# A head pair's logits and its A@V as ordered chains, rope's squares in one instruction, and a query projection in two parts

## The chip, the cores and the metric

The kernel runs on one core of a Trainium2 chip. The time is that of one execution on the device, in microseconds (us); the median of three runs is used. Lower is better.

## What is computed

Four layers of a decoder trunk on 256 tokens of width 1024, in float32. Each layer has a token mixer (layer 0 and 3: stick-breaking attention; 1: MoBA, which at 256 tokens is causal attention within one block; 2: a sliding window of 128 with two key heads and a learned sink per head) and a SwiGLU channel mixer, each behind an RMSNorm that is modulated by a vector c. There are 16 heads of width 64. Cut to what matters here:

```python
def stick_breaking_attention(h, w_in, w_out):
    q, k, v = jnp.split(h @ w_in, 3, axis=-1)
    z = einsum('bhqd,bhkd->bhqk', q, k) * scale
    log_beta = log_sigmoid(z)
    log_keep = where(past, log_sigmoid(-z), 0.0)
    later = cumsum(log_keep, axis=3, reverse=True) - log_keep
    a = where(past, exp(log_beta + later), 0.0)
    return merge_heads(einsum('bhqk,bhkd->bhqd', a, v)) @ w_out

def swa_sink_attention(h, w_in, qk_gain, sinks, w_out, cos, sin):
    q = apply_rope(rms_norm(q, qk_gain[0]), cos, sin)
    k = apply_rope(rms_norm(k, qk_gain[1]), cos, sin)
    ...
    m = maximum(max(s, axis=-1), sink)
    e = exp(s - m)
    p = e / (sum(e, axis=-1) + exp(sink - m))
    return merge_heads(p @ vb) @ w_out

for i in range(DEPTH):
    h = modulate(rms_norm(x, norm_gain[i, 0]), sh1, sc1)
    x = x + g1 * mixer[i % 3](h)
    h = modulate(rms_norm(x, norm_gain[i, 1]), sh2, sc2)
    x = x + g2 * swiglu(h, w_gate, w_up, w_down)
```

## The kernel before, in words

The layers run one after the other, each as projection, attention over eight pairs of heads, output projection, FFN. Products in float32 are made from two halves: a value is split into a rounded part (`hi`, `qkh`, `oth`; made on ScalarE) and the rest (`lo`, `qkl`, `otl`; made by a subtraction on VectorE), and three matmuls (hi by hi, lo by hi, hi by lo) are added up in PSUM (`mm3` with 256 columns, `tt3` with 512). Weights stream in as 1 MB pieces (`raw`) and are split in the same way by `prep` (L218 and L219, two halves of 128x1024 each); between them the modulation weights are multiplied by c on VectorE (L176, also 128x1024). Both of these serve later work: they are queued ahead of need at a low priority, and may stand anywhere among the attention's instructions.

One pair of heads in attention goes as follows. `scores` takes two PSUM buffers of tag `z` (there are two in all), one per head. Into each goes the mask (`identb` times the mask, L516; L518 in the sliding window, with 384 columns), and on top six matmuls for the logits (L523): three products of halves, each once for the first 128 queries (256 columns) and once for the rest (128 columns). A head's rows are 64 of the 128, the other head's the other 64. The source writes these alternating between the two heads.

- Stick-breaking (`sb_layer`): ScalarE makes Abs, Exp, Ln and Relu of `z` (L595 to L599), VectorE scans in two pieces (L601) and subtracts from the logits (L602), which is the last reader of `z`; ScalarE makes the exponential (L603).
- The other two (`softmax`): VectorE takes the maxima (L671, L672) and makes the bias `nb`, ScalarE the exponentials (L685, L686, the last readers of `z`), in the sliding window also the sink's (`es`, L682) ahead of them; VectorE makes the reciprocal and scales, ScalarE scales the rest (L691).
- `apply_v`, for the pair before: three transposes a head (L454) into a buffer `at`, a copy `aT` on ScalarE (L456), four matmuls A@V (L462: two heads by 256 and 128 columns) into `po`, and the split of the result (L470, L471).

MoBA and the sliding window also apply RMSNorm and rope to queries and keys (`rope`): one Square per head with the sum in its accumulator (L645), then products with the tables on VectorE. In the sliding window the queries come in two halves of 512 columns; `proj_q(1)`, the second, stands between the first and second pair and uses PSUM tags `at` and `o`, with 24 matmuls for each of two blocks of 128 tokens.

`out_proj` adds up the output projection for the first seven pairs' results as they come (in bank `wo`), and these matmuls fill TensorE between the logits.

Every engine takes its instructions in program order. What that order is, is decided by the framework's scheduler, which places each instruction where its own estimate has operands and buffers ready; the source's order is only its priority. `follow` adds a dependency that costs nothing at run time but forces an order of two instructions on one engine (matmul after matmul).

## Time and profile before

| | |
|---|---|
| median of 3 runs | 1260.95 us (1259.98 to 1266.66) |
| the profiled execution | 1266.64 us, its span 1264.9 us |
| TensorE (PE) busy | 1235.1 us, 98% |
| VectorE (DVE) busy | 1012.1 us, 80% |
| ScalarE (ACT) busy | 717.4 us, 57% |
| mean granted TensorE clock | 0.99 of full |

Times of the trace are microseconds from the span's start. A line `L523` is that of the source before. "Idle before" is how long an engine had nothing to run ahead of an instruction, and behind the arrow stands what released it. Rows of matmuls may be merged and overlap: an instruction's duration contains the way through the array, so that steps are read from start to start. In a window's row the clock is what was granted to TensorE on average (1.00 is 2.4 GHz, 0.50 is 1.2 GHz).

### The profile page before, as it was taken

To read this page: it belongs to the slowest core of one execution; us is meant where nothing else is said; L and a number is where in the kernel's file an instruction comes from. 1 tells how busy PE (TensorE), PEld (TensorE's weight loads), DVE (VectorE), ACT (ScalarE), POOL (GpSimd) and SP (SyncE) were. 2 spreads that over 40 slices of the span, in tenths; PEclk is the share of its full clock that TensorE was granted. 3 is DMA by queue.
4 is the path that set the end of the run, shared out by engine and by line. 5 is a ranking of instruction groups with operands and counts; after the bars stand their busy time and mean duration, and the time that the engine had idled before them with its cause. 6 is when DMAs were issued, how large, how long until landed. Compare 5 with 4: busy or idle time off the path is not lost.

```text
span 1264.9 us, 23755 instructions
## 1 busy us (share of the span) xinstructions
PE 1235.1 (98%) x9546; PEld 1159.9 (92%) x9546; DVE 1012.1 (80%) x1909; ACT 717.4 (57%) x1455; POOL 6.2 (0%) x28
## 2 busy tenths in 40 slices
PE   7999999999999999999998999999999999999998
PEld 5878999999977799999996689999998889999998
DVE  7989999898798769989879669887869876966542
ACT  4578565454478756545448676444446776644531
POOL 0000000000000000000000000000000000000000
PEclk9989999999999999999999899999999999999999
DMA  9966779988644227999864007987865641676530
GB/s 367 364 251 237 265 267 402 360 324 329 253 172 161 101 82 276 394 349 340 330 232 167 34 34 257 348 334 289 295 242 208 242 149 68 258 269 210 196 117 18
DMA packets 44033, 303.35 MB, mean 240 GB/s; under 512 B 5009, under 2 KB 6801, under 8 KB 7442
## 3 DMA queue, kind: packets, MB, share of 16 engines
q1 hardware_dynamic: 43922, 301.83, 64.0%
q8 instruction: 75, 1.23, 0.4%
q14 instruction: 36, 0.29, 0.1%
HBM read 300.76 MB, written 1.05 MB: 239 GB/s over the span
## 4 chain that ended last, share of the span: by engine, by line
PE 85%; DVE 8%; ACT 4%; issue 1%; DMA 1%; SPq 0%; DVEq 0%; ACTq 0%
PE ps_wo L382 8%; PE ps_wo L383 8%; PE ps_wo L381 8%; PE ps_z L381 8%; PE ps_z L382 8%; PE ps_z L383 8%; PE ps_pj L381 4%; PE ps_pj L382 4%; PE ps_pj L383 4%; PE ps_at L382 3%; PE ps_at L381 3%; PE ps_at L383 3%; PE ps_o L462 3%; DVE lo L219 3%; PE ps_z L523 3%; DVE raw L176 2%
## 5 line engine op out<-in xcount | busy, mean ns | idle before, releaser
L219 DVE TENSOR_TENSOR lo<-raw,hi 128x1024 fp32r<-128x1024 f32 x378 | 454.6, 1220 | 100.8 <-ACT hi L218 100.1
L218 ACT CAST hi<-raw 128x1024 fp32r<-128x1024 f32 x378 | 387.0, 1049 | 209.4 <-issue 50.6
L176 DVE SCALAR_TENSOR_TENSOR raw<-raw,cact 128x1024 f32<-128x1024 f32 x192 | 229.4, 1217 | 5.7 <-DMA raw<-ada 5.7
L381 PE MATMUL ps_z<-hh,hi 128*128 128x256 f32 x736 | 206.1, 280 | 0.0
L382 PE MATMUL ps_z<-hl,hi 128*128 128x256 f32 x736 | 205.8, 280 | 0.0
L383 PE MATMUL ps_z<-hh,lo 128*128 128x256 f32 x736 | 204.8, 278 | 0.0
L381 PE MATMUL ps_wo<-ahi,hi 128*128 128x256 f32 x704 | 199.2, 283 | 0.0
L382 PE MATMUL ps_wo<-alo,hi 128*128 128x256 f32 x704 | 199.2, 283 | 0.0
L383 PE MATMUL ps_wo<-ahi,lo 128*128 128x256 f32 x704 | 199.2, 283 | 0.0
L381 PE MATMUL ps_pj<-hh,hi 128*128 128x256 f32 x512 | 146.7, 287 | 2.4 <-DVE qkl L530 2.4
L382 PE MATMUL ps_pj<-hl,hi 128*128 128x256 f32 x512 | 145.5, 284 | 0.0
L383 PE MATMUL ps_pj<-hh,lo 128*128 128x256 f32 x512 | 144.3, 282 | 0.0
L382 PEld LDWEIGHTS ps_z<-hl,hi 128*128 128x128 f32 x736 | 139.1, 189 | 0.0
L381 PEld LDWEIGHTS ps_z<-hh,hi 128*128 128x128 f32 x736 | 138.3, 188 | 0.0
L383 PEld LDWEIGHTS ps_z<-hh,lo 128*128 128x128 f32 x736 | 138.2, 188 | 0.0
L382 PEld LDWEIGHTS ps_wo<-alo,hi 128*128 128x128 f32 x704 | 135.2, 192 | 0.0
L383 PEld LDWEIGHTS ps_wo<-ahi,lo 128*128 128x128 f32 x704 | 135.2, 192 | 0.0
L381 PEld LDWEIGHTS ps_wo<-ahi,hi 128*128 128x128 f32 x704 | 135.1, 192 | 0.0
L381 PEld LDWEIGHTS ps_pj<-hh,hi 128*128 128x128 f32 x512 | 98.1, 192 | 4.1 <-DVE qkl L530 2.8
L382 PEld LDWEIGHTS ps_pj<-hl,hi 128*128 128x128 f32 x512 | 98.8, 193 | 0.7
L383 PEld LDWEIGHTS ps_pj<-hh,lo 128*128 128x128 f32 x512 | 98.0, 191 | 0.1
L381 PE MATMUL ps_at<-hh,hi 128*128 128x256 f32 x336 | 94.0, 280 | 0.0
(220 smaller groups left out, 2405.6 us busy)
## 6 DMA issues: line engine op xcount, KB each, us to landing
raw<-wst SPq DMA_DIRECT2D x189, 1024.0 KB, 5.5
raw<-ada SPq DMA_DIRECT2D x96, 1024.0 KB, 6.2
x<-xin SPq DMA_DIRECT2D x4, 256.0 KB, 4.4
out<-x SPq DMA_DIRECT2D x8, 128.0 KB, 1.7
mraw<-masks SPq DMA_DIRECT2D x1, 256.0 KB, 6.6
ropec<-ropec SPq DMA_DIRECT2D x2, 128.0 KB, 4.5
early<-small SPq DMA_DIRECT2D x1, 128.0 KB, 2.1
qkg<-qkg SPq DMA_DIRECT2D x2, 64.0 KB, 4.9
```

The source lines that it names most:

```text
L176: filler("v", nc.vector.scalar_tensor_tensor(raw[:, j * D : (j + 1) * D], raw[:, j * D : (j + 1) * D], 1.0, cact, ALU.mult, ALU.mult, accu ...
L218: filler("s", nc.scalar.copy(hi[:, cols], raw[:, cols]))
L219: filler("v", nc.vector.tensor_sub(lo[:, cols], raw[:, cols], hi[:, cols].bitcast(F32)))
L381: first = nc.tensor.matmul(ps, whi, ahi, start=start, stop=False, skip_group_check=True)
L382: nc.tensor.matmul(ps, whi, alo, start=False, stop=False, skip_group_check=True)
L383: nc.tensor.matmul(ps, wlo, ahi, start=False, stop=stop, skip_group_check=True)
L462: last = nc.tensor.matmul(po[rows, cols], vf(j, 2 * pair + hh_), ats[hh_][:, src], start=j == 1, stop=j == 0, skip_group_check=True)
L523: nc.tensor.matmul(z[:, out], q[a][rows, tq], k[b][rows, tk], start=False, stop=b == 1, skip_group_check=True)
```

## The change

A helper `in_order` forces a list of instructions into that order. It is applied to the fourteen matmuls of a pair's masks and logits, and to the four of A@V. Other matmuls may still stand between them. Rope's squares become one Square over all heads and a reduction on VectorE. `proj_q` of the sliding window is called for one block of tokens at a time; the second half's two blocks stand behind the first pair's and the second pair's logits, in PSUM tags `wo`, and the first A@V comes behind the second of them.

```diff
+    def in_order(instructions):
+        for a, b in zip(instructions, instructions[1:]):
+            follow(a, b)
...
+        av = []
         for j, cols, src in ((1, slice(0, S), slice(P, 3 * P)), (0, slice(0, P), slice(0, P))):
             for hh_ in range(2):
                 rows = slice(hh_ * HD, (hh_ + 1) * HD)
-                last = nc.tensor.matmul(
+                av.append(nc.tensor.matmul(
                     po[rows, cols], vf(j, 2 * pair + hh_), ats[hh_][:, src], start=j == 1, stop=j == 0, skip_group_check=True
-                )
+                ))
+        in_order(av)
+        last = av[-1]
...
         zs = [ptile("z"), ptile("z")]
+        row = []
         for z in zs:
...
-                nc.tensor.matmul(z[:, 0 : 3 * P], identb, mask, start=True, stop=False, skip_group_check=True)
+                row.append(nc.tensor.matmul(z[:, 0 : 3 * P], identb, mask, start=True, stop=False, skip_group_check=True))
...
-                    nc.tensor.matmul(z[:, out], q[a][rows, tq], k[b][rows, tk], start=False, stop=b == 1, skip_group_check=True)
+                    row.append(nc.tensor.matmul(z[:, out], q[a][rows, tq], k[b][rows, tk], start=False, stop=b == 1, skip_group_check=True))
+        in_order(row)
         return zs
...
-        for h in range(n):
-            nc.scalar.activation(sq3[:, h, :], s3[:, h, :], AF.Square, accum_out=ss[:, h : h + 1])
+        nc.scalar.activation(sq3, s3, AF.Square)
+        nc.vector.tensor_reduce(ss[:, :n], sq3, AX.X, ALU.add)
...
-        def proj_q(n, tags):
-            ps = half_proj(wbase + 1 + 2 * n, hh, hl, tags)
-            for j in range(2):
-                r = small.tile([P, 8], F32, tag="rq", name="rq")
-                q[j, n] = rope(ps[j], 8, tab, j, 0, r)
-                nc.vector.tensor_scalar_mul(qs[:, j, 8 * n : 8 * n + 8], r, QK_SCALE)
+        def proj_q(n, tags, j):
+            ps = half_proj(wbase + 1 + 2 * n, hh, hl, tags, (j,))[0]
+            r = small.tile([P, 8], F32, tag="rq", name="rq")
+            q[j, n] = rope(ps, 8, tab, j, 0, r)
+            nc.vector.tensor_scalar_mul(qs[:, j, 8 * n : 8 * n + 8], r, QK_SCALE)
...
-        proj_q(0, ("wo", "wo"))
+        wo = ("wo", "wo")
+        for j in range(2):
+            proj_q(0, wo, j)
         turn(0)
         turn(1)
-        weights(0)
-        proj_q(1, ("at", "o"))
-        for p in range(1, 8):
+        for p in range(8):
             weights(p)
-            finish(p - 1)
-            if p < 3:
+            if p < 2:
+                proj_q(1, wo, p)
+            if p:
+                finish(p - 1)
+            if p in (1, 2):
                 turn(p + 1)
         out_proj(l, wbase + 5, lambda: finish(7))
```

All lines shift by 5 to 12, so that L219 is L224 in the changed kernel, L601 is L611 and L523 is L532. The number of instructions stays the same on TensorE; ScalarE has 86 fewer and VectorE 14 more. Since the scheduler runs over the whole program, instructions that the diff does not name move too.

TensorE, MoBA, the sixth pair (its `z` are 5030 and 5031 before, 4982 and 4983 after; `at` are transposes for the pair before it, `wo` the output projection). Before:

```order
L516 MATMUL ps_z_5030<-maskb_105,identb_104 128x2x128
L523 MATMUL ps_z_5030<-qkh_4958 128x256
L523 MATMUL ps_z_5030<-qkh_4958 128x128
L523 MATMUL ps_z_5030<-qkh_4958,qkl_4959 128x256
L523 MATMUL ps_z_5030<-qkh_4958,qkl_4959 128x128
L523 MATMUL ps_z_5030<-qkl_4959,qkh_4958 128x256
L523 MATMUL ps_z_5030<-qkl_4959,qkh_4958 128x128
L454 MATMUL ps_at_5071<-ident_103,a_4983 128x128
L516 LDWEIGHTS identb_104
L516 MATMUL ps_z_5031<-maskb_105,identb_104 128x2x128
L523 MATMUL ps_z_5031<-qkh_4958 128x256
```

and after:

```order
L459 MATMUL ps_at_5023<-ident_103,a_4935 128x128 x2
L387 MATMUL ps_wo_5172<-otl_4591,hi_4818 128x256
L459 MATMUL ps_at_5023<-ident_103,a_4935 128x128
L388 MATMUL ps_wo_5172<-oth_4590,lo_4819 128x256
L386 MATMUL ps_wo_5173<-oth_4590,hi_4826 128x256
L387 MATMUL ps_wo_5173<-otl_4591,hi_4826 128x256
L525 LDWEIGHTS identb_104
L525 MATMUL ps_z_4983<-maskb_105,identb_104 128x2x128
L532 MATMUL ps_z_4982<-qkh_4910 128x256
L532 MATMUL ps_z_4983<-qkh_4910 128x256
L532 MATMUL ps_z_4982<-qkh_4910 128x128
L532 MATMUL ps_z_4983<-qkh_4910 128x128
```

The heads now alternate (the first head's mask stands four rows ahead of this piece), and the transposes that stood between the heads have moved ahead of the second mask.

VectorE, first stick-breaking layer, from the sixth pair (`a_1115`, `a_1125`) to the first scan of the seventh (`a_1214`); `lo` is half a weight split, `raw` a modulation product, `x2` two of them. Before:

```order
L601 SCALAR_TENSOR_TENSOR a_1115<-a_1115,e_1111 128x128
L601 SCALAR_TENSOR_TENSOR a_1125<-a_1125,e_1121 128x256
L602 SCALAR_TENSOR_TENSOR a_1115<-ps_z_1095,a_1115 128x384
L601 SCALAR_TENSOR_TENSOR a_1125<-a_1125,e_1121 128x128
L219 TENSOR_TENSOR lo_1345<-raw_1138,hi_1344 128x1024
L602 SCALAR_TENSOR_TENSOR a_1125<-ps_z_1096,a_1125 128x384
L471 TENSOR_TENSOR otl_1191<-ps_o_1173,oth_1190 128x256
L176 SCALAR_TENSOR_TENSOR raw_1134,mod_133<-raw_1134,cact_85 128x1024 x2
L601 SCALAR_TENSOR_TENSOR a_1214<-a_1214,e_1210 128x256
```

and after:

```order
L611 SCALAR_TENSOR_TENSOR a_1115<-a_1115,e_1111 128x128
L181 SCALAR_TENSOR_TENSOR raw_1338,mod_133<-raw_1338,cact_85 128x1024
L612 SCALAR_TENSOR_TENSOR a_1115<-ps_z_1095,a_1115 128x384
L611 SCALAR_TENSOR_TENSOR a_1125<-a_1125,e_1121 128x256
L611 SCALAR_TENSOR_TENSOR a_1125<-a_1125,e_1121 128x128
L479 TENSOR_TENSOR otl_1191<-ps_o_1173,oth_1190 128x256
L612 SCALAR_TENSOR_TENSOR a_1125<-ps_z_1096,a_1125 128x384
L540 TENSOR_TENSOR qkl_1255<-ps_pj_1148,qkh_1254 128x512
L224 TENSOR_TENSOR lo_1361<-raw_1342,hi_1360 128x1024 x2
L181 SCALAR_TENSOR_TENSOR raw_1350,mod_133<-raw_1350,cact_85 128x1024
L181 SCALAR_TENSOR_TENSOR raw_1354,mod_133<-raw_1354,cact_85 128x1024
L611 SCALAR_TENSOR_TENSOR a_1214<-a_1214,e_1210 128x256
```

Three of the big instructions stood there, and five stand there now; over the seven such stretches of this layer it is 4, 4, 3, 4, 4, 3, 5 before and 5, 5, 5, 5, 5, 5, 4 after.

ScalarE, sliding window, the sixth pair (its sinks' exponentials are `es_8601` before, `es_8529` after), with the copies for the pair before it (`aT`) and that pair's A@V evacuation (`oth`). Before:

```order
L456 COPY aT_8632<-ps_at_8628 128x384
L456 COPY aT_8638<-ps_at_8634 128x384
L682 ACTIVATE es_8601<-nb_8598,sinks_106 128x2
L685 ACTIVATE a_8603,sm_8604<-ps_z_8579,nb_8598,qscale_7937 128x256
L686 ACTIVATE a_8603,sm_8604<-ps_z_8579,nb_8598,qscale_7937 128x128
L682 ACTIVATE es_8617<-nb_8614,sinks_106 128x2
L685 ACTIVATE a_8619,sm_8620<-ps_z_8580,nb_8614,qscale_7937 128x256
L691 ACTIVATE a_8603<-a_8603,sm_8604 128x128
L686 ACTIVATE a_8619,sm_8620<-ps_z_8580,nb_8614,qscale_7937 128x128
L470 CAST oth_8644<-ps_o_8627 128x256
L691 ACTIVATE a_8619<-a_8619,sm_8620 128x128
```

and after:

```order
L461 COPY aT_8560<-ps_at_8556 128x384
L701 ACTIVATE a_8480<-a_8480,sm_8481 128x128
L461 COPY aT_8566<-ps_at_8562 128x384
L478 CAST oth_8572<-ps_o_8555 128x256
L692 ACTIVATE es_8529<-nb_8526,sinks_106 128x2
L695 ACTIVATE a_8531,sm_8532<-ps_z_8507,nb_8526,qscale_7889 128x256
L696 ACTIVATE a_8531,sm_8532<-ps_z_8507,nb_8526,qscale_7889 128x128
L692 ACTIVATE es_8545<-nb_8542,sinks_106 128x2
L695 ACTIVATE a_8547,sm_8548<-ps_z_8508,nb_8542,qscale_7889 128x256
L701 ACTIVATE a_8531<-a_8531,sm_8532 128x128
L696 ACTIVATE a_8547,sm_8548<-ps_z_8508,nb_8542,qscale_7889 128x128
```

The evacuation `oth` of the pair before has moved from behind this pair's exponentials to ahead of them.

## Rows read from the trace of the kernel before

**Rows 1.** The page: busy time by engine, and the chain that ended last
```profile
PE 1235.1 (98%) x9546; PEld 1159.9 (92%) x9546; DVE 1012.1 (80%) x1909; ACT 717.4 (57%) x1455; POOL 6.2 (0%) x28
...
PE 85%; DVE 8%; ACT 4%; issue 1%; DMA 1%; SPq 0%; DVEq 0%; ACTq 0%
```

**Rows 2.** Busy time by stage: length, PE, PEld, DVE, ACT, POOL, clock, DMA share, GB/s
```profile
62.50:134.50 72.00, 67.54 (x482) 57.09 (x482) 67.77 (x120) 57.87 (x125) 0.00 (x0) 0.95 0.71 258
134.50:155.00 20.50, 20.50 (x157) 19.82 (x155) 17.85 (x49) 11.84 (x22) 0.00 (x0) 1.00 0.72 267
155.00:342.00 187.00, 187.00 (x1586) 186.97 (x1586) 167.64 (x277) 93.05 (x136) 3.01 (x12) 1.00 0.86 326
369.00:452.00 83.00, 81.65 (x521) 65.74 (x520) 61.52 (x180) 62.36 (x224) 0.00 (x0) 1.00 0.37 128
686.00:744.00 58.00, 52.70 (x304) 37.70 (x304) 36.45 (x160) 39.20 (x143) 0.00 (x0) 0.85 0.15 55
```

**Rows 3.** TensorE in time, MoBA, an early pair: start, us, instruction group, [idle before]
```profile
384.10 0.38 PE L516 MATMUL ps_z<-maskb,identb 128*128 128x256 bf16 x2
384.41 0.45 PE L523 MATMUL ps_z<-qkh 64*128 64x256 f32 x4
...
385.25 0.50 PE L387 MATMUL ps_wo<-hi,hh 128*128 128x512 f32 x1
```

**Rows 4.** TensorE in time, MoBA, a late pair, and the start of the next
```profile
430.02 0.28 PE L516 MATMUL ps_z<-maskb,identb 128*128 128x256 bf16 x1
430.24 0.44 PE L523 MATMUL ps_z<-qkh 64*128 64x256 f32 x2
...
431.07 0.33 PE L454 MATMUL ps_at<-ident,a 128*128 128x128 f32 x1
...
432.27 0.76 PE L454 MATMUL ps_at<-ident,a 128*128 128x128 f32 x5
...
435.21 0.28 PE L516 MATMUL ps_z<-maskb,identb 128*128 128x256 bf16 x1
```

**Rows 5.** TensorE in time, SWA: an A@V and the first masks of two pairs
```profile
726.31 0.86 PE L462 MATMUL ps_o<-aT,vkv 128*64 128x256 f32 x6
...
728.04 0.34 PE L518 MATMUL ps_z<-maskb,identb 128*128 128x384 bf16 x1
...
734.02 0.34 PE L518 MATMUL ps_z<-maskb,identb 128*128 128x384 bf16 x1
```

**Rows 6.** Groups of VectorE, SB0: name, shapes, count, busy us, mean ns, idle before
```profile
L176 DVE SCALAR_TENSOR_TENSOR raw<-raw,cact 128x1024 f32<-128x1024 f32 x21 | 25.1, 1211 | 0.0
```

**Rows 7.** VectorE in time, SB0: first scans, longest wait, last pair's scans
```profile
69.02 1.01 DVE L601 TENSOR_TENSOR_SCAN a<-a,e 128x256 f32<-128x256 f32 x2 [0.75 <-ACT e L597]
...
84.71 0.42 DVE L471 TENSOR_TENSOR otl<-ps_o,oth 128x256 fp32r<-128x256 f32 x1 [2.51 <-ACT oth L470]
...
127.44 1.58 DVE L601 TENSOR_TENSOR_SCAN a<-a,e 128x256 f32<-128x256 f32 x3
```

**Rows 8.** TensorE in time, SWA: the second pair's logits begin and are over
```profile
692.24 0.48 PE L518 MATMUL ps_z<-maskb,identb 128*128 128x384 bf16 x1 [4.34 <-ACT a L686]
...
695.50 1.54 PE L454 MATMUL ps_at<-ident,a 128*128 128x128 f32 x6
```

**Rows 9.** Busy time and clock, SWA around the first maximum
```profile
689.80:700.00 10.20, 7.76 (x31) 4.97 (x30) 9.00 (x38) 5.52 (x18) 0.00 (x0) 0.50 0.47 192
```

**Rows 10.** ScalarE in time, SWA, one pair of the steady run
```profile
725.34 0.48 ACT L456 COPY aT<-ps_at 128x384 f32<-128x384 f32 x1
725.72 0.30 ACT L682 ACTIVATE es<-nb,sinks 128x2 f32<-128x2 f32 x1
...
728.35 0.38 ACT L470 CAST oth<-ps_o 128x256 fp32r<-128x256 f32 x1
```

**Rows 11.** Groups of MoBA: rope's square on ScalarE, the larger maximum on VectorE
```profile
L645 ACT ACTIVATE rsq<-ps_wo 128x64 f32<-128x64 f32 x32 | 6.6, 233 | 1.2 <-PE ps_wo L389 1.2
...
L671 DVE TENSOR_REDUCE mx<-ps_z 128x1 f32<-128x256 f32 x16 | 6.7, 416 | 0.6 <-PE ps_z L523 0.6
```

More of the change, by code (lines that the diff above doesn't have):

```diff
@@ L515, in scores @@
                 out = z.rearrange("p (a c) -> p a c", a=2)[:, :, 0:P]
-                nc.tensor.matmul(out, identb, mask.unsqueeze(1).to_broadcast([P, 2, P]), start=True, stop=False, skip_group_check=True)
+                row.append(nc.tensor.matmul(out, identb, mask.unsqueeze(1).to_broadcast([P, 2, P]), start=True, stop=False, skip_group_check=True))
             else:
-                nc.tensor.matmul(z[:, 0 : 3 * P], identb, mask, start=True, stop=False, skip_group_check=True)
+                row.append(nc.tensor.matmul(z[:, 0 : 3 * P], identb, mask, start=True, stop=False, skip_group_check=True))
         for a, b in ((0, 0), (1, 0), (0, 1)):
```

## The prediction

> **What bounds the kernel now.** I read the page first: TensorE is busy for 98% of the span and the chain that ended last runs on it for 85%, on VectorE for 8% [rows 1]. A saving on TensorE is therefore worth its full size in most places, and the question is whether the edited stages are such places. So I cut the span into stages [rows 2]. The FFN stages (155 to 342 is one of four) and the output projection at 134.5 keep TensorE busy without a break; the diff does not reach into the former. What is edited lies in the attention stages. There the picture differs by stage. In the first one (stick-breaking, 62.5 to 134.5; "SB0" below) VectorE has 67.77 us of work in 72.00 and TensorE 67.54: both are near full. In MoBA's (369 to 452) TensorE has 81.65 of 83.00 and VectorE only 61.52: TensorE alone bounds it. In the sliding-window one (686 to 744, "SWA") TensorE has 52.70 of 58.00, at a mean granted clock of 0.85. The last stick-breaking stage has all of its eight pairs alternating already, in the order of before and of after, so I give it 0.
>
> **What the edit is worth on TensorE.** The timeline shows both forms of a pair's logits side by side. One of MoBA's early pairs already alternates between the heads: two masks and twelve logits take 384.10 to 385.25, 1.15 us [rows 3]. A late pair goes head by head: 430.02 to 432.27, less one transpose of about 0.11, is 2.14 us [rows 4]. The difference is 1.0 us a pair: the six logits of one head alone take 0.83 us (430.24 to 431.07 [rows 4]), and the twelve of the alternating pair 0.84 (384.41 to 385.25 [rows 3]), so two heads' 64-row matmuls run at once when they stand next to each other. By the order of before and after, the number of pairs that change is six in SB0, three in MoBA, six to seven in SWA. A@V chained alone brings 0.0 to 0.2 us a pair where it was torn apart, mostly in SB0 and MoBA's early pairs; I count 0.3 in all, and only where TensorE bounds.
>
> **MoBA.** The last three pairs gain up to 1.0 us each. The chain through the logits does not stop this: a pair needs the maximum (0.42 us for the larger reduction [rows 11]) and two heads' exponentials before the next pair's logits, which I add up to 4.8 us a cycle from the same operations' durations in SWA [rows 10], against 5.2 between these pairs now (430.02 to 435.21 [rows 4]). So 0.4 is sure and 1.0 possible, each: -1.2 to -3.2. I take **-2.5**, near the upper end, since TensorE has queued output-projection work to fill with. Rope's squares: the eight 64-wide ones cost 0.233 us each [rows 11], 1.9 us together; for the one 512-wide Square I take 0.6, a third more than the 384-wide copy of 0.48 [rows 10]. The reduction it adds on VectorE is new: between 0.42 (256 wide, one row [rows 11]) and twice that; I take 0.65. MoBA's VectorE has 21 us to spare, so it costs **0**; cover gone, 0.65 for each of the ropes on the path.
>
> **SB0.** Here the sum turns round. VectorE waits 2.51 us at 84.71 and little else [rows 7], it does not wait for logits, so 6 us less on TensorE only make TensorE wait for VectorE: the next pair's mask may not start until both heads' buffers are free, which VectorE's L602 does last. What counts is the number of big instructions (the weight splits of L219 and the modulation products of L176, both 1.21 us [rows 6], 1.14 from start to start) that stand between the first scan of the first pair and that of the last. The order has 27 of them before and 34 after: seven more, drawn from ahead of the first scan and from behind the last. Seven times 1.14 is +8.0. Against it stands VectorE's idle time in that stretch (69.02 to 127.44), 3.3 us with two shorter waits, which the fuller queue can swallow: +4.7. Behind the last scans one big instruction falls away for a few small ones: -0.8. That gives **+3.9**, rounded to +4. It is covered by nothing: the output projection behind it is full (20.50 of 20.50 [rows 2]) and begins with what the last pair leaves. Ends: 0, if the three instructions drawn forward only take time in which VectorE would stand anyway; +7 if the old idle time comes back, or a modulation product waits for its weights.
>
> **SWA.** Three places, in order. First pair: VectorE, busy for 9.00 of 10.20 us around the first maximum [rows 9], decides when it comes; two weight splits fewer ahead of it (2 x 1.14) and four reductions more (two of 0.65, two narrow ones I estimate at 0.2) make it 0.6 to 1 us earlier: -0.8. Second pair: before, TensorE stood for 4.34 us until the exponential at L686 let go of the buffer, then needed 692.24 to 695.50 for two serial heads, at 0.50 of full clock [rows 8, 9]. The second query half's matmuls (48 of them) are now split: 17 stand in that wait. The wait itself does not vanish, since all that work was done ahead of it before; it moves ahead, to where the first pair's rope is not ready. What is gained is the block, 3.26 against 1.15 (full clock) or 2.1 (half): -1.6. Third to fifth pairs: from 695.50 to the fifth pair's logits it takes 23.0 us now (the start at 728.04 less two periods of 5.98 [rows 5], plus a serial block of 2.4, MoBA's 2.14 with masks half as wide again). After, each step is a chain: maximum and bias 1.1, the exponentials 2.6 from the sink's (725.72) to the end (728.35 [rows 10]), masks and logits 1.2, hence 4.9 at least; and where ScalarE has the pair before's A@V evacuation ahead of the sink's exponential, transposes (0.55 for three; five take 0.76 [rows 4]), copy (0.48 [rows 10]), A@V (0.86 [rows 5]) and evacuation (0.38 [rows 10]) come in place of the 1.1, hence 6.0; with a query cast or a rope's square too, 7.5 to 7.8. By the order the three are 7.8, 7.5 and 5.3: 20.6, -2.4. Last three pairs: **6.0 against 5.98 now**: nothing gained, because before, the first head's maximum ran under the second head's logits, and now it doesn't. Sum -4.8. TensorE then idles some 1.3 us in each of these cycles, and the clock was at 0.50 for 10.20 us of this stage as it is [rows 9]; for a further loss of that kind I add 0.8: **-4**. Ends -8 (the half clock goes altogether) and +2.
>
> The page "TensorE: Matmul & The Clock Gate" of the Trainium skill, Part 1, says that the gate sets the clock by how busy the array has lately been. That rule speaks against this change: by it the sum would be that of the second rival below, by the bare count of work the one that follows.
>
> **Sum.** 4 - 2.5 - 4 - 0.3 = -2.8 us. The profiled execution spans 1264.9 and took 1266.64; the median is 1260.95, so I carry the difference over: **1258.2 us**. A measurement of this kernel tells about 0.5% (6.3 us) from no change; this is below it.
>
> **Rivals.**
> 1. *VectorE doesn't bind SB0.* Six pairs at 1.0 less would be -6; I allow -4 for those that are half alternating already. For it: TensorE and VectorE are within 0.3 us of each other there [rows 2]. Against it: the count of 34. Then -4 - 2.5 - 4 - 0.3 = -10.8, **1250.2**.
> 2. *The clock falls where TensorE now waits.* Place: SWA's last four cycles. For it: after the wait of 4.34 the granted clock was 0.50 until 700 [rows 8, 9]. Price: transposes, A@V and logits on the chain, 2.5 us a cycle, double: 4 x 2.5 = +10, SWA +6 in place of -4, in all +7.2, **1268.2**, slower. It decides from the third such cycle on. Against it: waits of under 1 us left the clock alone in MoBA (TensorE 81.65 of 83).
> 3. *The chain changes little.* The two masks stand apart in after, with transposes and projections between them, so that buffers and not TensorE set the pace everywhere, and SB0's additional work falls into waits: SB0 0, MoBA -1, SWA 0: **1260**.
>
> **How the numbers follow.** Forecast 0.45, rival 1 0.24, rival 2 0.17, rival 3 0.14. Faster by over 0.5% (under 1254.6) is rival 1 and a corner of the forecast with SWA's -8: 0.28. Slower by over 0.5% (above 1267.3) is most of rival 2 and a corner of SB0's +7: 0.19. Within: 0.53. The range runs from rival 1's time to just below rival 2's: 1250 to 1268; the forecast's own is 1253 to 1265.
>
> **What would show it.** Right: SB0's attention 3 to 5 us longer, VectorE without a pause of 2 us in it, TensorE with some 10 us of pauses, most of them ended by the statement that is L602 now; MoBA's last three pairs under 5 us apart; SWA's last four pairs 6.0 us apart with pauses of TensorE of over 1 us; FFN stages the same within 0.5. Wrong: SB0's attention shorter than 72 (rival 1), the granted clock in the changed kernel's SWA lower than 0.85 (rival 2), or MoBA's last pairs still 5.2 apart (rival 3).

## The result: 1274.16 us, slower, and the profile after

The changed kernel takes 1274.16 us (median of 6 runs, 1273.13 to 1276.41), against 1263.86 of before in all 6 of its runs (1259.98 to 1266.71): a ratio of 1.0078, 95% interval 1.0052 to 1.0105. It is slower by more than this kernel's measurement leaves open, and outside the range of the prediction. Of before's runs three lie at 1260.0 to 1261.3 and three at 1266.4 to 1266.7, the profiled one (1266.64) among the upper, and in its later runs, listed with their mean granted clock, all under 1263 us had 0.993 to 0.997 of full and all above 1263.6 had 0.985 to 0.992. After's profiled run took 1273.16. Between the two profiles lie 6.5 us, between the medians 10.3.

The page of the kernel after, its busy times and the chain that ended last, beside [rows 1] (the page counts a square's read of its accumulator as an instruction too, hence 186 fewer on ScalarE):

```profile
PE 1225.6 (96%) x9546; PEld 1148.3 (90%) x9546; DVE 1019.6 (80%) x1923; ACT 704.8 (55%) x1269; POOL 6.5 (1%) x28
...
PE 82%; DVE 11%; ACT 4%; issue 2%; DMA 1%; SPq 0%; DVEq 0%; ACTq 0%
```

TensorE's busy time fell by 9.5 us while the time rose: the matmuls did get cheaper. VectorE's share of the chain went from 8 to 11%. The stages of the kernel after, beside [rows 2] (length, PE, PEld, DVE, ACT, POOL, clock, DMA share, GB/s; the attention windows are SB0, MoBA and SWA from the first logits on):

```profile
62.50:139.90 77.40, 65.07 (x482) 52.43 (x482) 73.14 (x146) 58.15 (x124) 0.00 (x0) 0.93 0.75 284
139.90:160.40 20.50, 20.49 (x155) 19.64 (x154) 12.30 (x22) 11.85 (x22) 0.00 (x0) 1.00 0.31 104
160.40:347.40 187.00, 187.00 (x1585) 186.94 (x1585) 167.79 (x276) 92.91 (x136) 0.99 (x4) 1.00 0.87 325
374.30:455.20 80.90, 80.31 (x523) 63.52 (x522) 65.56 (x188) 57.19 (x150) 0.00 (x0) 1.00 0.39 141
691.70:751.00 59.30, 50.16 (x329) 35.42 (x329) 39.88 (x165) 41.28 (x133) 0.00 (x0) 0.94 0.16 54
```

SB0 is 5.4 us longer, and VectorE has 73.14 of its 77.40 us filled. What it does more there it does less of in the output projection behind, 12.30 us in place of 17.85, where TensorE was the bound and VectorE had room. FFN is 187.00 as before. MoBA is 2.1 shorter. SWA did not get shorter, though its mean clock here is 0.94 against 0.85.

For every kernel run, the table gives the attention stages (from the first mask to the end of the last A@V, in the profiled run), the median and the ratio to the runs of before on the same chip. SB1 is the last, stick-breaking stage.

| kernel | SB0 | MoBA | SWA | SB1 | median us | ratio [95%] |
|---|---|---|---|---|---|---|
| before | 69.57 | 82.30 | 70.06 | 82.87 | 1263.86 | 1 |
| after | 75.08 | 80.17 | 73.83 | 82.33 | 1274.16 | 1.0078 [1.0052, 1.0105] |
| chain_sb | 77.37 | 82.29 | 67.38 | 82.48 | 1271.90 | 1.0072 [1.0047, 1.0097] |
| chain_moba | 68.36 | 80.44 | 70.21 | 82.45 | 1260.88 | 0.9972 [0.9954, 0.9989] |
| chain_softmax | 68.43 | 80.40 | 71.25 | 82.45 | 1264.93 | 1.0027 [1.0011, 1.0044] |
| chain_av | 68.20 | 82.43 | 66.45 | 82.11 | 1265.72 | 1.0017 [0.9995, 1.0039] |
| rope_only | 68.39 | 82.47 | 71.62 | 82.44 | 1262.73 | 0.9997 [0.9976, 1.0018] |
| split_only | 68.40 | 82.40 | 67.13 | 81.70 | 1259.87 | 0.9970 [0.9956, 0.9985] |
| after_oldq | 75.74 | 80.17 | 75.24 | 82.66 | 1275.52 | 1.0093 [1.0062, 1.0124] |
| after_atq | 76.86 | 80.17 | 71.81 | 82.82 | 1275.58 | 1.0075 [1.0046, 1.0104] |
| after_oldsq | 74.51 | 80.35 | 74.52 | 82.38 | 1275.09 | 1.0087 [1.0064, 1.0111] |
| light_before | 65.96 | 82.41 | 66.37 | 80.36 | 1258.04 | 0.9961 [0.9943, 0.9979] |
| light_chain | 63.92 | 82.44 | 70.09 | 81.20 | 1258.86 | 0.9959 [0.9937, 0.9980] |
| softmax_oth | 66.87 | 80.44 | 65.79 | 81.54 | 1258.21 | 0.9962 [0.9946, 0.9978] |
| after_nosb_oth | 66.84 | 80.15 | 70.92 | 83.24 | 1262.72 | 0.9999 [0.9982, 1.0017] |
| oth_split | 67.58 | 80.40 | 64.22 | 81.40 | 1257.72 | 0.9942 [0.9916, 0.9968] |
| oth_split_wo | 69.33 | 80.31 | 68.32 | 82.48 | 1262.19 | 0.9994 [0.9978, 1.0010] |

Ten of these kernels have before's order in SB0 and its whole work (chain_av its order but for A@V), and there the stage took 66.84 to 69.57, 68.2 in the mean; the five with chained logits and unchanged work took 74.5 to 77.4, 75.9 in the mean. The chain's price in SB0 is thus 7.7 us, of which the two first profiles show 5.5: before's stage was 1.4 above its mean, with a stretch of half clock in it, and after's 0.8 below. SWA with before's order took 66.4 to 70.2 in six kernels, 68.4 in the mean.

### The profile page after: what moved, and what is told of

It reads as the page before. It is cut to its first block, busy times and chain, and to the rows that moved or that the text cites. A ratio compares the mean times of both kernels' runs of the same rounds, so it can differ in the third digit from the quotient of the medians.

```text
span 1271.4 us, 23577 instructions
## 1 busy us (share of the span) xinstructions
PE 1225.6 (96%) x9546; PEld 1148.3 (90%) x9546; DVE 1019.6 (80%) x1923; ACT 704.8 (55%) x1269; POOL 6.5 (1%) x28
## 4 chain that ended last, share of the span: by engine, by line
PE 82%; DVE 11%; ACT 4%; issue 2%; DMA 1%; SPq 0%; DVEq 0%; ACTq 0%
PE ps_wo L386 8%; PE ps_wo L388 8%; PE ps_wo L387 8%; PE ps_z L387 7%; PE ps_z L386 7%; PE ps_z L388 7%; PE ps_pj L386 4%; PE ps_pj L387 4%; PE ps_pj L388 4%; DVE lo L224 3%; PE ps_at L387 3%; PE ps_at L386 3%; PE ps_at L388 3%; DVE raw L181 3%; PE ps_o L468 2%; PE ps_wo L392 2%
## 5 line engine op out<-in xcount | busy, mean ns | idle before, releaser
L224 DVE TENSOR_TENSOR lo<-raw,hi 128x1024 fp32r<-128x1024 f32 x378 | 454.6, 1220 | 97.5 <-ACT hi L223 96.6
```

Of the source, the lines that this page charges most:

```text
L224: filler("v", nc.vector.tensor_sub(lo[:, cols], raw[:, cols], hi[:, cols].bitcast(F32)))
```

## The experiments

**One part each: the logits' chain by stage.**

chain_sb is before with the chain in stick-breaking logits alone:

```diff
+        if mask is strict_b:
+            in_order(row)
```

> The kernel before, with only the masks and logits of the two stick-breaking layers chained; everything else as before. In the first such layer its order on VectorE has 34 big instructions between the first scans (27 before), as the changed kernel has. Theory (VectorE bounds that layer, the surplus big instructions are the cost): the whole of the changed kernel's loss there, last A@V at 139 to 140 us in place of 134.35, total +4 to +6 us. Rival (the loss comes from another part of the change, or from the pair-wide wait on both logit buffers, and the surplus is harmless): last A@V within 2 us of 134.35, total within 2 us.

SB0 is 77.37 against 69.57, and MoBA stayed at 82.29. By its ratio (1.0072, some 9 us, more than the 4 to 6 expected) this part alone costs nearly as much as the whole change; what the other parts lose and gain comes near to cancelling.

chain_moba is the same with `if mask is causal_b:`.

> The kernel before, with only MoBA's masks and logits chained. Theory (TensorE bounds MoBA, so a pair's saving of 1.0 us counts for the last three pairs): MoBA from its first mask to its last A@V 2 to 3 us shorter than 82.0, all else the same, total -2 to -3 us. Rival (buffers pace it, and the changed kernel's 2 us there came from rope's squares in one instruction): MoBA within 0.7 us, total within 1 us.

MoBA 80.44 against 82.30 and a ratio below 1 with its whole interval: this part by itself is a gain of some 3.5 us by the ratio, 1.9 by the stage.

chain_softmax has `if mask is not strict_b:`, MoBA and the sliding window.

> The kernel before, with MoBA's and the sliding window's masks and logits chained, all else as before. Against the kernel with MoBA's alone it differs in the sliding window only. Theory (there the A@V evacuation stands ahead of the next sink's exponential, and TensorE waits and loses its clock): the steady step 6.1 to 6.3 us in place of 5.98, the tail 0.5 to 2 longer, the layer 3 to 6 us longer than 70, total 2 to 6 us over the MoBA-only kernel. Rival (the loss there is from rope's one Square and the split of the second query half): layer within 1 us of 70.

MoBA's gain stays; SWA is 71.25 against 70.06, and the total 1.0027: the chain in SWA gives back what MoBA gained. The stage is longer by 1.2 us, not by the 3 to 6 expected; its last three steps hold 0.6 of that and the tail 0.8. The first masks of three successive pairs there (TensorE in time, chain_softmax):

```profile
719.15 0.34 PE L526 MATMUL ps_z<-maskb,identb 128*128 128x384 bf16 x1
...
725.23 0.32 PE L526 MATMUL ps_z<-maskb,identb 128*128 128x384 bf16 x1
...
731.40 0.32 PE L526 MATMUL ps_z<-maskb,identb 128*128 128x384 bf16 x1
```

They are 6.08 and 6.17 apart, against 5.98 in [rows 5]: two heads at once in place of one after the other, and the cycle is longer, not shorter, as expected.

chain_av chains the A@V alone (`in_order(av)`).

> The kernel before with only the four A@V matmuls of a pair chained. Theory (worth 0.0 to 0.2 us a pair where TensorE bounds): every stage within 0.5 us of before, total within 1.5 us. Rival (an order that the scheduler had chosen for a reason is lost): a stage over 1 us longer.

SB0 and SWA are 1.4 and 3.6 us shorter than in before's profile, more than the 0.5 expected, but both lie within what this order takes (66.8 to 69.6 and 66.4 to 70.2). The total is 1.0017 with 1 inside the interval, so nothing that the chain is worth could be measured.

**Is it VectorE's work in SB0?** light_before and light_chain cut the modulation products of layer 0 that fall into the attention stage to 64 of their 1024 columns (the rest of that sum is left out), one without and one with chain_sb's edit:

```diff
+        W = 64 if l == 0 and i >= KT else D
...
-                raw[:, j * D : (j + 1) * D], raw[:, j * D : (j + 1) * D], 1.0, cact,
+                raw[:, j * D : j * D + W], raw[:, j * D : j * D + W], 1.0, cact[:, :W],
```

> The kernel before, with the modulation products of layer 0 that lie in its attention cut from 1024 to 64 columns (the rest of that sum is left out, so the modulation is not the reference's). This takes some 1.07 us from each of about 20 instructions on VectorE. Theory (VectorE bounds the first stick-breaking layer, also before): from the first mask to the last A@V 62 to 66 us in place of 69.6. Rival (the wait for the two logit buffers paces it): 68 to 70 us.

> The kernel before with the stick-breaking layers' masks and logits chained, and with the same modulation products cut to 64 columns (the rest of that sum is left out). Theory (with VectorE relieved, TensorE and the chain bound the layer, and the chained logits then pay): first mask to last A@V 3 to 6 us shorter than in the kernel with the cut alone. Rival (waiting for both buffers of a pair is itself the cost): as long or longer than it.

With VectorE relieved the sign turns: 65.96 without the chain, 63.92 with it, from one profile each. (The totals are alike; in the profiled runs light_chain's SWA was 70.09 and light_before's 66.37, where both have before's order and lie within what it takes.) The stage's windows, light_before first, then light_chain, then chain_sb for comparison (columns as above):

```profile
65.10:131.10 66.00, 63.20 (x475) 52.89 (x474) 48.77 (x141) 55.18 (x120) 0.00 (x0) 1.00 0.83 316
```

```profile
65.20:129.20 64.00, 57.27 (x475) 48.32 (x474) 48.88 (x141) 55.12 (x120) 0.00 (x0) 1.00 0.85 326
```

```profile
65.10:142.60 77.50, 68.11 (x475) 54.88 (x475) 70.84 (x141) 55.90 (x120) 0.00 (x0) 0.87 0.71 270
```

DVE falls from 70.84 to 48.88 us by the cut, and the same chain that cost 7.7 us now gains 2.0. So it is VectorE's work between the scans that the chain turns into time. The cut moved the order as well: between the first scans stand 31 products and splits in light_before and 34 in light_chain, of which 20 and 22 are the small ones. The gain is smaller than the 3 to 6 expected: TensorE has 6.73 us of pauses in light_chain against 2.80 in light_before. Of these 4.2 and 1.2 are ended by the statement that frees the two logits buffers, so the wait for both of them takes back a part of the gain. It is not what made the loss: with VectorE's work whole, that statement ended 1.6 us of pauses in before and 2.2 in chain_sb.

**The sliding window.** rope_only has the one Square and the reduction, split_only the new loop and `proj_q`; all else as before.

> The kernel before, with only rope's eight squares as one and the reduction on VectorE. Theory (VectorE decides when the first logits of the sliding window come, and four reductions stand ahead of them): first logits 0.5 to 1 us later than 14.1, MoBA within 0.5 us of 82.3, total within 2 us of before. Rival (ScalarE's shorter row of squares pays): first logits earlier than 14.1, MoBA shorter by more than 0.5 us.

> The kernel before, with only the sliding window's second query half in two pieces, behind the first and the second pair, in buffers wo. Theory (the pieces wait for the buffer wo that rope of the first half still reads; the work is moved, not saved): first logits end 15.5 to 16.5 us after that pair's masks (14.1 before), the step to the second pair shorter by about as much, both together 21.3 to 22.5 (21.8 before); layer 67 to 72 us, total within 3 us of before. Rival (a piece in the long wait saves what it takes, 4 us): both together 17 to 19 us, total -3 to -5 us.

rope_only came out as expected (first logits 0.74 us later, MoBA and total as before). split_only did not: its first step is 14.32 where 15.5 to 16.5 was expected, and it gained (0.9970).

After_oldq, after_atq and after_oldsq are the kernel after with one part undone: the second query half whole and ahead of the first A@V; split, but in the old buffers; the eight squares.

```diff
-                proj_q(1, wo, p)
+                proj_q(1, ("at", "o"), p)
```

> The changed kernel, with the sliding window's second query half put back: one piece between the first and second pair, in buffers at and o. Theory (the second half's matmuls wait for the buffer wo that rope of the first half still reads, and the first logits stand behind them at half the clock): first logits end 13 to 14 us after the pair's masks, as before (13.9; 16.3 in the changed kernel), and total 2 to 4 us under the changed kernel. Rival (the chained logits themselves are what delays the layer): first logits as late as in the changed kernel, total within 1 us of it.

> The changed kernel, with the sliding window's second query half split as it is there, but its two pieces in buffers at and o in place of wo. Theory (the wait for wo): no wait of 2.7 us at the first of these matmuls, first logits 2 to 5 us earlier than in the changed kernel, total 2 to 5 us under it. Rival (the split itself, that is the transposes for the first logits behind a part of the second half, is what costs): first logits as late, total within 1 us of the changed kernel.

> The changed kernel with rope's eight squares put back. Theory (rope's reductions on VectorE delay the transposes and lengthen the wait before the second half's pieces, after which the clock is lower; without them the split costs next to nothing): in the sliding window first logits end 14.0 to 15.2 us after the masks, against 16.5 in the changed kernel, and the total 1 to 4 us under the changed kernel. Rival (the split together with the chained logits is enough): first logits at 16 to 17, total within 1 us of the changed kernel.

None of the three undone parts brought the total down (1.0093, 1.0075 and 1.0087 against 1.0078), against all three expectations: by the totals, no single part of SWA's change carries the loss there. What they do show is read step by step. The table gives us and, behind @, the mean granted clock: from the first mask to the end of the first pair's logits, from there to the end of the second's, and so on, and from the last logits to the last A@V's end.

| SWA | first | second | third | fourth | fifth | sixth | seventh | eighth | tail |
|---|---|---|---|---|---|---|---|---|---|
| before | 14.14 | 7.66 @.62 | 10.13 @.67 | 8.29 @.73 | 4.62 | 5.98 | 5.98 | 5.99 | 7.25 |
| after | 16.46 @.79 | 5.71 | 11.09 @.82 | 8.10 @.82 | 5.37 | 6.69 | 6.17 | 6.17 | 8.07 |
| after_oldq | 14.88 | 7.07 @.54 | 9.41 @.80 | 7.07 | 6.69 | 6.17 | 6.85 @.88 | 8.13 @.50 | 8.97 @.88 |
| after_atq | 14.91 | 7.07 @.58 | 8.14 @.74 | 7.28 @.94 | 5.79 @.78 | 6.70 | 6.18 | 6.17 | 9.57 @.76 |
| after_oldsq | 14.49 @.76 | 6.10 | 8.04 | 11.77 @.71 | 6.85 | 6.17 | 6.17 | 6.18 | 8.75 @.91 |
| chain_softmax | 14.10 | 7.56 @.68 | 7.36 @.87 | 6.89 @.85 | 8.73 @.73 | 6.18 | 6.18 | 6.17 | 8.07 |
| rope_only | 14.88 | 7.70 @.72 | 11.33 @.50 | 7.61 @.69 | 6.52 | 5.72 | 4.62 | 5.98 | 7.26 |
| split_only | 14.32 @.76 | 5.98 | 7.44 | 10.29 | 5.53 | 5.71 | 4.62 | 5.98 | 7.25 |
| softmax_oth | 14.15 | 7.54 @.62 | 7.99 @.50 | 7.06 @.76 | 5.37 | 5.37 | 5.37 | 5.37 | 7.56 |
| oth_split | 14.11 | 7.55 @.59 | 6.98 @.71 | 6.30 | 5.61 | 5.37 | 5.37 | 5.37 | 7.55 |
| oth_split_wo | 14.22 @.76 | 6.10 | 8.16 @.97 | 10.57 @.70 | 5.60 | 5.37 | 5.38 | 5.38 | 7.54 |

(A step without @ had 1.00, or .99.) Three things follow. First, the new rope makes the first step 0.74 longer by itself, and undone in after it gives 1.97 back (16.46 to 14.49). That 1.97 is not the squares' duration but TensorE's order: the second half's matmuls begin 6.54 us behind the first mask in after and 6.95 in after_oldsq, so the wait for their buffer ends no later, but 21 of the 48 stand ahead of the first logits in after and 13 in after_oldsq, eight more of 0.23 to 0.43 us each. Yet after_oldsq's total is not better: its fifth step, its tail, and its third and fourth together took more than it gained. Secondly, first and second step together go by that count: with the split in `wo` they are 20.3 to 20.6 where 13 matmuls stand ahead (split_only, oth_split_wo, after_oldsq), 22.17 in after and 22.69 in after_nosb_oth where 21 do; before has 21.80, and the new rope with the old buffers 21.95 to 21.98. So the split helped here only with the eight squares, by the order that came with them. Thirdly, in the rows of this table with the split in `wo` (after, after_oldsq, split_only, oth_split_wo), the third or the fourth step takes 10.3 to 11.8, in split_only at full clock; with the split in the old buffers neither is over 8.2. The totals show this only partly: oth_split and oth_split_wo differ by 0.5% with intervals apart, after and after_atq do not differ.

**Which of ScalarE's instructions sets the steady step?** softmax_oth is chain_softmax with the evacuation of the pair before (`oth`) held behind this pair's last exponential, in SWA alone:

```diff
-            nc.scalar.activation(a[:, S : S + P], z[:, S : S + P], AF.Exp, ...)
+            last_exp = nc.scalar.activation(a[:, S : S + P], z[:, S : S + P], AF.Exp, ...)
+            state["exp"] = last_exp if sink is not None else None
...
+        evac = nc.scalar.copy(hi, po[:, :S])
+        if state.get("exp") is not None:
+            follow(state["exp"], evac)
```

> As the kernel with MoBA's and the sliding window's logits chained, and in addition the evacuation of the pair before's A@V is held behind this pair's exponentials on ScalarE in the sliding window. Theory (the order on ScalarE sets the chained step): steady step 5.0 to 5.5 us in place of 6.17, the layer 2.5 to 4 us shorter than without it. Rival (the step is set by something else, TensorE or VectorE): 6.0 to 6.2 as without it.

The first masks of three successive pairs (TensorE in time), and ScalarE around one evacuation:

```profile
709.49 0.34 PE L528 MATMUL ps_z<-maskb,identb 128*128 128x384 bf16 x1
...
714.85 0.34 PE L528 MATMUL ps_z<-maskb,identb 128*128 128x384 bf16 x1
...
720.23 0.34 PE L528 MATMUL ps_z<-maskb,identb 128*128 128x384 bf16 x1
```

```profile
715.30 0.20 ACT L699 ACTIVATION_READ_ACCUMULATOR a<-ps_z,nb,qscale 128x1 f32 x1
715.39 0.37 ACT L477 CAST oth<-ps_o 128x256 fp32r<-128x256 f32 x1
```

The step is 5.36 to 5.38 where it was 6.08 to 6.17, and SWA as a whole 65.79 where it was 71.25. The evacuation starts without a wait as the exponentials end. It was the evacuation's place in ScalarE's order that set the step, as expected.

**Putting the good parts together.** after_nosb_oth is after without the chain in stick-breaking and with that hold; oth_split is softmax_oth with the second query half split in its old buffers, oth_split_wo the same in `wo`.

> The changed kernel, without the chain of the stick-breaking layers' logits, and with the A@V evacuation held behind the next exponentials in the sliding window. Theory (these two places are the whole loss): first stick-breaking layer 67 to 70 us as before, MoBA 80.2, sliding window 66 to 70, steady step there 5.4, total 3 to 7 us under before. Rival (another part of the change costs as well): total no less than before.

> The kernel before with MoBA's and the sliding window's logits chained and the evacuation held behind the exponentials, and in addition the second query half in two pieces in buffers at and o. Theory (a piece of the second half keeps TensorE from its wait of 4 us and so at the full clock): sliding window 62 to 65.5 us against 65.8 without the pieces, granted clock over 0.8 in its first steps. Rival (work is only moved): 65.5 to 68 us.

> The kernel before with MoBA's and the sliding window's logits chained, the evacuation held behind the exponentials, and the second query half in two pieces in buffers wo. It differs from the one with at and o in the buffers alone. Theory (the split in wo alone made the first two steps 20.3 us together, in at and o 21.7, since it keeps the wait of 4 us away): sliding window 61.5 to 64 us against 64.2, total 5 to 9 us under the kernel before. Rival (the wait comes back elsewhere): 64 to 67 us.

after_nosb_oth does not gain (0.9999), against what was expected. Its late steps are 5.38, but its first and third take 16.99 and 10.85: the new rope and the split in `wo` give back what the hold gains. oth_split has the lowest median here: 1257.72 us, 0.9942 [0.9916, 0.9968], below before with its whole interval, though not told apart from softmax_oth (0.9962 [0.9946, 0.9978]). SWA is the 64.22 expected, but not because the clock held: it was 0.59 and 0.71 in the second and third step, where over 0.8 was expected. oth_split_wo lost most of the gain (0.9994, SWA 68.32 for 61.5 to 64), against what was expected: the buffers `wo` are not the better place for the split.

## Why the prediction was wrong, step by step

**SB0, +4: the right mechanism and sign, too small.** The term rested on the seven additional big instructions between VectorE's first scan of the first pair and that of the last. The order has 34 in all kernels with this chain and 27 in the ten of before's order. VectorE in time, after, beside [rows 7]:

```profile
68.84 1.01 DVE L611 TENSOR_TENSOR_SCAN a<-a,e 128x256 f32<-128x256 f32 x2 [0.65 <-ACT e L607]
...
82.74 2.36 DVE L224 TENSOR_TENSOR lo<-raw,hi 128x1024 fp32r<-128x1024 f32 x2 [0.39 <-ACT hi L223]
...
132.35 1.00 DVE L611 TENSOR_TENSOR_SCAN a<-a,e 128x256 f32<-128x256 f32 x2
```

From first to last scan it is 63.51 us, against 58.42: +5.1 where 4.7 was the sum, with 0.69 us of idle time left, so in this profile the old wait of 2.51 was indeed swallowed. Pair by pair the clean part is the last four: their steps add up to 30.64 us before (7.18 to 8.41 each) and 35.71 after (8.40 to 9.33), +5.1, all at a clock of 1.00. Two things were missing. One is the tail, TensorE in time:

```profile
132.95 1.54 PE L468 MATMUL ps_o<-aT,v 128*64 128x256 f32 x6 [2.25 <-ACT aT L461]
```

From the last of the statements that was L602 to the end of the last A@V it takes 5.03 us, before 3.78: TensorE stood for 2.25 us, and from the last logits on the granted clock was 0.69 in the mean (0.68 or 0.69 in all five kernels with this chain). The other is the reference: before's own third step was 10.97 us at 0.69, where kernels of the same order without that stretch need 8.25. The sum took a disturbed stage for the normal one; against the mean of ten it is +7.7. With that falls the term of 3.3 us taken off for idle time. VectorE's busy time from the first to the last pair's first scan is 54.8 to 54.9 us in all ten and 62.6 to 62.9 in the five, the 8.0 of the seven instructions but for 0.1; its idle time there is 2.2 us in the mean of the ten and 1.6 in that of the five. So 0.5 us was swallowed, not 3.3. The pauses of TensorE (12.3 us) came as foretold, but half of them, 6.3, are ended by ScalarE's copy of the weights for A@V (L461) and 2.3 by the statement I had named. The first rival, that VectorE doesn't bind SB0, is refuted by chain_sb. Its mechanism is what light_chain shows once VectorE's work is gone.

**MoBA, -2.5: right in size, wrong in place.** The stage lost 2.1 us, in chain_moba alone 1.9. But the pairs did not move together. The first masks of the late pairs (TensorE in time, after):

```profile
435.17 0.28 PE L525 MATMUL ps_z<-maskb,identb 128*128 128x256 bf16 x1
...
440.79 0.28 PE L525 MATMUL ps_z<-maskb,identb 128*128 128x256 bf16 x1
...
446.35 0.28 PE L525 MATMUL ps_z<-maskb,identb 128*128 128x256 bf16 x1
```

They are 5.62 and 5.56 apart, not under 5 and not the 5.19 of [rows 4]. TensorE has 80.31 of 80.90 us filled: the time saved in the logits let output-projection matmuls move up between the pairs (48 of them before the last logits are over, 25 in before), and what stands behind the last logits shrank from 9.56 to 6.84 us. Here, where TensorE is full, the saved work shows at the end of the stage and not in the step.

**SWA, -4: the step that failed; it measured +3.8.** Against the mean of the six kernels with before's order (68.4) it is +5.4. What failed first is the premise that VectorE decides when the first pair comes: TensorE's own queue did. By its parts, with the table above:

- First and second pair, -2.4 in the sum, measured 22.17 against 21.80, +0.4. The second step is 5.71, as good as meant; the first, where I had put -0.8, is +2.3. The rows (TensorE in time, after, then VectorE, then the window):

```profile
680.27 0.55 PE L709 MATMUL ps_pj<-ident,kdup 128*128 128x128 f32 x3 [2.74 <-DVE kdup L810]
...
683.57 0.77 PE L392 MATMUL ps_wo<-hi,hh 128*128 128x512 f32 x1 [2.75 <-DVE rsq L663]
684.13 0.63 PE L393 MATMUL ps_wo<-lo,hh 128*128 128x512 f32 x1
...
690.34 0.49 PE L709 MATMUL ps_pj<-ident,roped 128*128 128x128 f32 x3
...
691.68 0.45 PE L532 MATMUL ps_z<-qkh 64*128 64x256 f32 x4
```

```profile
691.49 0.69 DVE L540 TENSOR_TENSOR qkl<-ps_pj,qkh 128x512 fp32r<-128x512 f32 x1 [3.10 <-ACT qkh L539]
```

```profile
680.00:689.00 9.00, 5.98 (x16) 4.55 (x17) 8.34 (x18) 0.92 (x3) 0.00 (x0) 0.64 0.48 157
```

  TensorE waits 2.74 us for the keys, then 2.75 for VectorE to be done reading the first half's product (L663, in rope), since the second half's first block now wants that `wo` buffer. Then 21 of the second half's 48 matmuls run ahead of the first logits, the early ones at 0.43 us from start to start in place of the 0.23 of full clock; the clock was 1.00 from 680.3 to 682.0 and 0.50 from 682.5 to 689.0. Three of the four transposes for the first logits (690.34) stand behind 17 of them, and the first logits behind these. VectorE, done with that rope at 688.4, waits 3.10 us for what follows from them. In the sum I had counted the work that moves ahead, and said that it would stand where rope is not ready; I had not asked which buffer it would wait for, how much of it would stand ahead of the first logits, and at which clock it would run. By the Trainium skill ("TensorE: Matmul & The Clock Gate", Part 1) the clock gate goes by how busy the array has lately been; these rows agree, with 0.64 granted in a window that holds the end of one wait and the whole of another.
- Third to fifth pair, -2.4 in the sum (20.6), measured 24.56 against 23.04, +1.5. The fifth is 5.37, where the chain said 5.3. The third is 11.09 where it said 7.8, the fourth 8.10 for 7.5. In chain_softmax, which has neither split nor new rope, the third and fourth are 7.36 and 6.89, under the chain's figures, but the fifth is 8.73, and the three make 22.98: even there the 2.4 does not show. In after the third step begins with the second half's last ten matmuls (2.4 us), then TensorE waits twice for the exponentials that free the logits' buffers, and the clock is 0.50 from 706.5 to 713:

```profile
703.42 0.32 PE L527 MATMUL ps_z<-maskb,identb 128*128 128x384 bf16 x1 [0.93 <-ACT a L696]
...
705.50 0.32 PE L527 MATMUL ps_z<-maskb,identb 128*128 128x384 bf16 x1 [1.76 <-ACT a L696]
```

  after_atq, which differs from after in the buffers alone, took 21.21 for the three at a mean clock of 0.82 (after 0.86). So most of what is over comes with the split in `wo` and not with the clock; which of these waits makes it stays open.
- Last three, 0 in the sum, measured +1.1; and the tail, not in the sum, +0.8. The steady step was put at 6.0 and is 6.17, one of the three 6.69. One cycle of it, TensorE in time and then ScalarE (beside [rows 5, 10]):

```profile
734.00 0.32 PE L527 MATMUL ps_z<-maskb,identb 128*128 128x384 bf16 x1
...
738.99 0.39 PE L386 MATMUL ps_wo<-oth,hi 128*128 128x256 f32 x1 [0.46 <-ACT oth L478]
...
740.17 0.32 PE L527 MATMUL ps_z<-maskb,identb 128*128 128x384 bf16 x1
741.05 0.52 PE L459 MATMUL ps_at<-ident,a 128*128 128x128 f32 x3 [0.56 <-DVE a L700]
```

```profile
730.96 0.48 ACT L461 COPY aT<-ps_at 128x384 f32<-128x384 f32 x1 [0.98 <-PE ps_at L459]
...
732.39 0.37 ACT L478 CAST oth<-ps_o 128x256 fp32r<-128x256 f32 x1 [0.95 <-PE ps_o L468]
732.66 0.30 ACT L692 ACTIVATE es<-nb,sinks 128x2 f32<-128x2 f32 x1
```

  ScalarE waits 0.95 us for the pair before's A@V, evacuates it, and only then starts the next pair's exponentials, as the prediction's chain had it. softmax_oth proves it by taking the evacuation away from there.

The allowance of 0.8 for the clock was not the size of the matter either: the second rival's price, the half clock in the last cycles, did not fall due in after (1.00 there). In after_oldq's profile it did (TensorE in its last step, 7.74 of 8.20 us filled at half clock):

```profile
736.50:744.70 8.20, 7.74 (x37) 5.37 (x36) 3.46 (x16) 4.27 (x15) 0.00 (x0) 0.50 0.01 4
```

**Rope's squares: sized well, placed wrongly.** The groups of MoBA, after, beside [rows 11], the reduction and the Square:

```profile
L655 DVE TENSOR_REDUCE ss<-rsq 128x8 f32<-128x512 f32 x5 | 3.4, 683 | 0.6 <-ACT rsq L654 0.6
L654 ACT ACTIVATE rsq<-ps_wo 128x512 f32<-128x512 f32 x4 | 2.4, 593 | 1.2 <-PE ps_wo L394 1.2
```

0.68 and 0.59 us for the 0.65 and 0.6 taken. In MoBA this cost nothing, as said. In SWA's first step, where VectorE is full (8.34 of 9.00 us in the window above), it did stand on the path: 0.74 in rope_only, about the 0.65 put for a rope without cover. The larger loss of after's first step is the order of TensorE that came with it.

**A@V, -0.3.** It can't be told from nothing (chain_av).

**From the profile to the median.** The sum was made against a profiled run of 1266.64 and its distance to the median, -5.7, carried over. That distance was no constant of the kernel. Most of it lies in where half-clock stretches had fallen in before's SB0 and SWA: in chain_av's profile (1261.06), of the same order but for A@V, these two stages are 1.4 and 3.6 us shorter, 5.0 of the 5.6 us between the two. After's profiled run lies 1.0 us below its median. Of the 16.0 us between forecast and result, 9.3 are in the difference of the two profiles (-2.8 by the sum, +6.5 measured) and 6.7 in this step.

**The rivals.** The second came nearest in time (1268.2), with the wrong place: SWA did get slower, but at its beginning and by ScalarE's order, and SB0 carried the larger part. Its own sign, a clock in SWA under 0.85, did not come (0.94); and in before the clock had been at half from 689.9, while the wait of 4.34 was still on, and not only after it. The third, that little changes, is refuted by chain_sb and chain_moba, whose intervals leave 1 out on either side.

## What to carry to other kernels

Chaining matmuls so that they overlap pays where TensorE is full (MoBA), and costs where another engine's queue is the bound: count first what the new order puts between that engine's instructions on the path. When work is split and moved forward, ask for each piece which buffer it needs and who still reads it, since a wait there can hold up everything queued behind, and count how much of it stands ahead of what the path needs next. And before a sum is carried from one profiled run to a median, see whether that run's stages are as long as they usually are.

## What the runs showed of the hardware

- The same instruction order ran with its half-clock stretch at different places. In SB0's third step, ten kernels of one order took from 8.25 us at 1.00 to 10.97 at 0.69 with all later steps the same to 0.04 us. That alone moves a stage by 2.7 us. In SWA, three kernels of before's order took 66.4 to 67.4 us and three 70.1 to 70.2.
- In after the granted clock fell to half within the second of two waits of 2.74 and 2.75 us on TensorE, and at the end of one of 2.25 (0.50 from 682.5 to 689.0 and from 133.0 to 139.7); the steady cycles with several waits of about 0.5 us each (15.75 of 18.60 us busy) kept 1.00.
- Relieving VectorE of 22 us in one stage turned an edit on TensorE from a loss of 7.7 us (a difference of means) to a gain of 2.0 (one profile each), with both engines near full before.
